# Walking the columns of matmuls in other orders, in five stages of an encoder trunk

## The chip, the cores and the metric

The kernel runs on one core of one Trainium2 chip. The metric is the device time of one execution in microseconds. It runs as one program that covers two whole layers and the final norm.

## The reference

Two layers of an encoder on a sequence of 512 tokens with 1024 features, in float32. Each layer mixes tokens in three branches, merges them, and then does a SwiGLU feed-forward and a gated per-layer embedding:

```python
for i in range(DEPTH):
    h = rmsnorm(x, mix_norm[i])
    z = h @ w_in[i]
    ...                      # recurrent branch, latent attention, forgetting attention
    merged = g[:, :, 0] * y_a + g[:, :, 1] * y_b + g[:, :, 2] * y_c
    x = x + merged @ w_o[i]
    hf = rmsnorm(x, ffn_norm[i]) @ w_gate_up[i]
    x = x + (jax.nn.silu(hf[..., :D_FF]) * hf[..., D_FF:]) @ w_down[i]
    pg = jax.nn.sigmoid(rmsnorm(x, ple_norm[i]) @ w_ple_gate[i])
    x = x + pg * (p[i] @ w_ple[i])
return rmsnorm(x, final_norm)
```

The parts that the change touches are the last three products of a layer: `w_gate_up` (1024 to 2 x 2816 features), `w_down` (2816 to 1024), and `w_ple` (256 to 1024) with `w_ple_gate` (1024 to 1024).

## The kernel before

Activations are kept feature-major: 128 features on the partitions, the 512 tokens along the columns. A dense product (`dense`, L246) takes one of the eight PSUM banks, 128 output features by 512 tokens of float32, and adds to it over k, the blocks of 128 input features. To keep float32 accuracy, weights and activations are each split in two float32r parts, hi and lo, and each k makes three matmuls (`mm3`, L239): hi x hi, hi x lo, lo x hi. The weights are the stationary operand, 128 x 128; the moving operand is a page of 512 tokens. All of it goes through `mm` (L236), whose `nc.tensor.matmul` is L237 of the profile. A page (`pr`) is 1024 contiguous columns per partition, hi in the first 512 and lo in the last; a bank is 512 contiguous columns. So each matmul of a dense product reads 512 neighbouring columns and adds to 512 neighbouring columns, first to last.

The weights come as a stream in the order of their use: 256 KB units of four tiles by DMA from SyncE, split by ScalarE (L112) and VectorE (L113) into a ring of five units (`hl`). When a product is done, VectorE and ScalarE read its bank whole and in order and give it back.

The feed-forward (`ffn`) runs 22 pairs of gate and up products, each 8 k blocks of three matmuls, 1056 matmuls in all; then 8 down products of 22 k blocks, 528 matmuls. The embedding (`ple`) runs 8 products of 2 k blocks and 8 of 8, 240 matmuls of 512 columns; in the second layer it ends in `ple_last`, whose gate products take 256 tokens at a time. A norm's 1/rms is summed by four one-column matmuls against a column of ones and spread over the partitions by two matmuls of 512 columns (`norm_bcast`, L332) that run among the first products of the next stage. `trunk` calls `mix`, `ffn` and `ple` for each layer. The order of the work is set by a scheduler, from the order of the code and the dependencies of tiles.

Of the kernel before, what the change touches and what calls it, by code (L numbers as in the profile page):

```python
# [26 lines left out]
# columns of w_in  # L27
# [3 lines left out]
# columns of the small per-partition vectors, per layer  # L31
V_MIX, V_FFN, V_PLE, V_GB, V_CW, V_CB, V_BA, V_BX, V_QN, V_KN, V_BF = (
    0, 8, 16, 24, 48, 64, 68, 72, 76, 79, 81)
NV = 82
V_LAM = DEPTH * NV          # lambdas of all layers, side by side
# [3 lines left out]
NUNITS = 606                # units of four 128x128 weight tiles in the stream  # L39
KEPT = NUNITS - 16          # from here on the stream is kept on chip: it is used twice  # L40
PACKED = (8, 9, 311, 312)  # units whose tiles hold the parts of 64 columns side by side


class Pages:
    """Pages of one tile, handed out oldest-freed first."""
# [39 lines left out]
class Stream:  # L85
    """The weights, in the order in which TensorE uses them: loaded ahead, split into two
    float32r parts that sum to the float32 value."""
# [46 lines left out]
    def tile(self, spec):  # L134
        """hi and lo of the next 128x128 tile"""
        u, k = divmod(self.pos, 4)
        if k == 0:
            self._ensure(u)
        self.spec.append(spec)
        self.pos += 1  # L140
        return self._parts(u, slice(128 * k, 128 * k + 128))

    def again(self, i):
        """tile i of the stream, one of those that were kept"""
        return self._parts(i // 4, slice(128 * (i % 4), 128 * (i % 4) + 128))
# [6 lines left out]
    def wide(self, spec):  # L152
        """hi and lo of a 128x512 tile, at the start of a unit"""
        self.align()
        u = self.pos // 4
        self._ensure(u)
        self.spec += [(spec, i) for i in range(4)]
        self.pos += 4
        return self._parts(u)

# [6 lines left out]
class Trunk:  # L167
    def __init__(self, ctx, tc, wst, vec, xT, pT, trig, masks, outT, last):
        self.tc, self.nc = tc, tc.nc
        self.a_vec, self.a_x, self.a_p, self.a_trig, self.a_masks, self.a_out, self.a_last = (  # L170
            vec, xT, pT, trig, masks, outT, last)
        nc = self.nc
        pool = ctx.enter_context(tc.tile_pool(name="sb", bufs=1))
        ps = ctx.enter_context(tc.tile_pool(name="ps", bufs=1, space=bass.MemoryType.PSUM))
        dr = ctx.enter_context(tc.tile_pool(name="dr", bufs=1, space=bass.MemoryType.DRAM))
        NR, NF, NRAW, NHL = 31, 20, 4, 5
        raw = pool.tile([128, NRAW * 512], F32, name="raw")
        hl = pool.tile([128, NHL * 1024], F32R, name="hl")
        self.w = Stream(tc, wst, raw, hl, NRAW, NHL)
        self.pr = Pages(pool.tile([128, NR * 1024], F32R, name="pr"), NR, 1024, "float32r")  # L180
        self.w.pages = self.pr
        self.raw = raw
        self.pf = Pages(pool.tile([128, NF * 512], F32, name="pf"), NF, 512, "float32")
        self.tmp = self.pf
        self.banks = Banks([ps.tile([128, 512], F32, name=f"bank{i}") for i in range(8)])
        self.pth = pool.tile([128, 1664], F32R, name="pth")
        self.ptl = pool.tile([128, 1664], F32R, name="ptl")
        self.identr = pool.tile([128, 128], F32R, name="identr")
        self.ident = self.identr[:, :].bitcast(F32)
        self.fmask = pool.tile([128, 128], F32, name="fmask")  # L190
        self.onesr = pool.tile([128, 128], F32R, name="onesr")
        self.one = pool.tile([128, 2], F32, name="one")
        self.eps = pool.tile([128, 2], F32, name="eps")
        self.vec = pool.tile([128, NVEC], F32, name="vec")
        self.sp = pool.tile([128, DEPTH * 4], F32, name="sp")
        self.msp = pool.tile([128, DEPTH * 4], F32, name="msp")
        self.small = pool.tile([128, 96], F32, name="small")
        self.xs = dr.tile([KD, 128, SEQ], F32, name="xs")
        self.chunk = dr.tile([4, 2 * SEQ], F32R, name="chunk")
        self.small_at = 0  # L200
        self.defer = None

    # -- small things ---------------------------------------------------------------------

    def cols(self, n):
        """n columns of a ring of small per-partition values"""
        if self.small_at + n > 96:
            self.small_at = 0
        s = self.small_at
        self.small_at += n  # L210
        return self.small[:, s:s + n]
# [24 lines left out]
    def mm(self, out, a, b, start, stop):  # L236
        self.nc.tensor.matmul(out, a, b, start=start, stop=stop, skip_group_check=True)  # L237
# [6 lines left out]
    # -- products, as generators that stop after every k tile -----------------------------  # L244

    def dense(self, spec, xs, evac, m=128):  # L246
        """out[m, tokens] = sum over k of W[k, m] * X[k, tokens]; xs are pages"""
# [11 lines left out]
    def group(self, specs, xs, evacs):  # L259
        """several of them side by side, k tile by k tile"""  # L260
# [20 lines left out]
    # -- RMSNorm ---------------------------------------------------------------------------  # L281

    def norm_add(self, st, x):
        """adds the squares of x (128 features) to the sums of norm st"""
# [17 lines left out]
    def norm_sum(self, st, n, fold=None):  # L302
        """token-major 1/rms, times fold, and its diagonal for the broadcast"""
# [10 lines left out]
        # 1/sqrt(v): a first value from the bits of v, good to 2e-3, and three Newton steps  # L314
# [30 lines left out]
    def normed(self, x, g):  # L345
        """page with both parts of x * g"""
        p = self.pr.take()
        self.ts(p.h, x, g)
        self.stt(p.l, x, g, p.h.bitcast(F32), ALU.mult, ALU.subtract)
        return p  # L350

    def after_norm(self, st, n, gen, s1, s2):
        """the first products after a norm, whose results wait for it; the sums are taken after
        s1 of their steps and the broadcast after s2"""
# [11 lines left out]
    # -- set-up -----------------------------------------------------------------------------  # L366

    def log1p_exp_neg(self, out, t1, t2, u, e):
        """out = log1p(s) / 2 with s = exp(-|u|), as atanh(y) with y = s / (2 + s)"""
# [11 lines left out]
    def setup(self):  # L381
# [11 lines left out]
        # TensorE's clock rises while it is busy  # L393
# [30 lines left out]
        # softplus(-lambda), times 2  # L424
# [9 lines left out]
    # -- mixers -------------------------------------------------------------------------------  # L434
# [4 lines left out]
    def mix(self, layer):  # L439
# [6 lines left out]
        # recurrent branch  # L446
# [39 lines left out]
        # rotary key and forget logits  # L486
# [12 lines left out]
        def rope(z, src, out_h, out_l, m):  # L499
            """z may be src"""  # L500
# [8 lines left out]
        def key_and_forget():  # L509
            """the rotary key, and the sums of the log forget gates; both parts of the weights side  # L510
            by side, so that one pass serves both"""
# [33 lines left out]
        # attention pieces  # L545
        qp, kp = {}, {}

        def ev_heads(pages, p, r, fox, is_q):
            """two heads' queries or keys to their pages, times 1/rms unless r is None"""
            f8 = 0.125 if fox and is_q else 1.0  # L550

            def f(b):
# [21 lines left out]
                for e in range(2):  # L574
# [3 lines left out]
                    if fox:  # L578
                        # queries [hi, hi | lo, extra], keys [hi, lo | hi, extra] or [lo, hi | hi, extra]
# [26 lines left out]
        def values(spec, X, rT):  # L606
            """token-major values: page per token tile, [head][hi 64 | lo 64]"""
# [23 lines left out]
        # recurrence: gates, then the scan  # L631
# [32 lines left out]
        def lru_tail():  # L664
            # one change of ScalarE's tables for all of them
# [23 lines left out]
        def renorm(*ks):  # L689
            """x * g / rms, for the products from here on"""  # L690
# [17 lines left out]
        # merge  # L708
# [39 lines left out]
        # attention  # L748
        def attention(fox, odd, plan, tail):
            """plan[p]: products (with their count of k tiles) to run beside head pair p; tail: a  # L750
            generator that runs beside the last steps"""
# [118 lines left out]
        # second phase products: latent projections  # L870
# [60 lines left out]
        def place_rope(p):  # L931
            """after the pair's pages are there"""
# [47 lines left out]
        # latent attention  # L980
# [24 lines left out]
        # output projection, residual, next norm  # L1005
# [22 lines left out]
    def ffn(self, layer):  # L1028
# [36 lines left out]
        self.st, self.xp = {}, []  # L1065

# [70 lines left out]
    def ple_last(self, X, pw):  # L1137
        """the last of them, and the final norm, by halves of the tokens"""
# [32 lines left out]
        def finish(js):  # L1171
            """the first half, by features"""
# [12 lines left out]
        def turn(j, x):  # L1185
            """the second half, by tokens: x times the final gain, to be transposed, and the squares"""
# [70 lines left out]
@with_exitstack  # L1257
def trunk(ctx, tc, *aps):
    t = Trunk(ctx, tc, *aps)
    t.setup()  # L1260
    for layer in range(DEPTH):
        t.mix(layer)
        t.ffn(layer)
        t.ple(layer)
    assert (t.w.pos + 7) // 8 * 2 == NUNITS, f"the stream has {t.w.pos} tiles"
    return t


# [85 lines left out]
def _masks():  # L1354
    """the causal mask of a diagonal block; and the chunk mask as a product of rank 4: row r is one
    for the queries in the first half of token tile r, and -1e30 for the keys in its second half"""
# [33 lines left out]
```

## Time and profile before

| | us |
|---|---|
| median of 2 runs | 1826.52 |
| the runs | 1824.92 and 1828.12 |
| span of the profiled execution, first to last instruction | 1825.0 |
| TensorE busy | 1807.5 |
| VectorE busy | 1210.6 |
| ScalarE busy | 817.1 |

The profiled execution's time is its span and the little that lies around it; the span stands 1.5 us under the median of the runs. Matmuls are pipelined, so the duration of one (392 ns in the mean) is longer than the distance between the starts of two, and busy TensorE time is not a measure of its rate; the rate is read from starts. In the names of the profile, `bank` is PSUM, `pr` are pages of two float32r parts, `pf` pages of float32, `hl` the split weights, `onesr` and `one` constants. PE is TensorE, DVE is VectorE, ACT is ScalarE.

### The profile page before, as it was taken

To read this page: it belongs to the slowest core of one execution; us is meant where nothing else is said; L and a number is where in the kernel's file an instruction comes from. 1 tells how busy PE (TensorE), PEld (TensorE's weight loads), DVE (VectorE), ACT (ScalarE), POOL (GpSimd) and SP (SyncE) were. 2 spreads that over 40 slices of the span, in tenths; PEclk is the share of its full clock that TensorE was granted. 3 is DMA by queue.
4 is the path that set the end of the run, shared out by engine and by line. 5 is a ranking of instruction groups with operands and counts; after the bars stand their busy time and mean duration, and the time that the engine had idled before them with its cause. 6 is when DMAs were issued, how large, how long until landed. Compare 5 with 4: busy or idle time off the path is not lost. (4 is left out here: it accounts for less than half of the span.)

```text
span 1825.0 us, 24155 instructions
## 1 busy us (share of the span) xinstructions
PE 1807.5 (99%) x8490; PEld 1505.6 (82%) x8490; DVE 1210.6 (66%) x2421; ACT 817.1 (45%) x1562; POOL 117.2 (6%) x234
## 2 busy tenths in 40 slices
PE   9999999999999999999999999999999999999998
PEld 8778888888888888888887788888888888888887
DVE  8997678866665555444778966888576555553457
ACT  4766556553333333223447655565533333332243
POOL 1220001100000000000103200010000000000000
PEclk9999999999999999999999999999999999999999
DMA  5232223324222222322333322242232222232231
GB/s 178 91 131 82 81 78 117 97 72 139 96 95 96 96 98 98 110 94 97 133 110 122 106 81 82 91 116 85 87 128 92 99 98 97 95 109 99 98 116 47
DMA packets 98826, 184.17 MB, mean 101 GB/s; under 512 B 13552, under 2 KB 14752, under 8 KB 98704
## 3 DMA queue, kind: packets, MB, share of 16 engines
q1 hardware_dynamic: 89280, 162.04, 25.7%
q0 software_dynamic: 8416, 19.45, 3.8%
q8 instruction: 66, 1.08, 0.2%
q10 hardware_dynamic: 1008, 1.14, 0.2%
q14 instruction: 56, 0.46, 0.1%
HBM read 173.98 MB, written 4.21 MB: 98 GB/s over the span
## 5 line engine op out<-in xcount | busy, mean ns | idle before, releaser
L237 PE MATMUL bank<-pr,hl 128*128 128x512 f32 (+1 forms) x6812 | 1602.9, 392 | 2.8 <-ACT pr L233 1.1
L237 PEld LDWEIGHTS bank<-pr,hl 128*128 128x128 f32 (+1 forms) x6812 | 1269.9, 188 | 267.3 <-ACT pr L233 2.0
L112 ACT CAST hl<-raw 128x512 fp32r<-128x512 f32 x590 | 364.3, 618 | 672.0 <-PE bank L237 403.8
L113 DVE TENSOR_TENSOR hl<-raw,hl 128x512 fp32r<-128x512 f32 x590 | 404.2, 686 | 378.6 <-ACT hl L112 360.4
L221 DVE TENSOR_TENSOR pf<-pf 128x512 f32<-128x512 f32 (+3 forms) x235 | 151.1, 651 | 31.8 <-ACT pf L230 29.9
L221 DVE TENSOR_TENSOR pf<-bank,pf 128x512 f32<-128x512 f32 (+3 forms) x198 | 132.8, 676 | 58.6 <-PE bank L237 32.1
L230 ACT ACTIVATE pf<-pf 128x512 f32<-128x512 f32 (+1 forms) x145 | 86.1, 600 | 112.7 <-DVE pf L221 110.5
L237 PE MATMUL bank<-pr 128*128 128x256 f32 (+5 forms) x704 | 120.7, 303 | 4.1 <-ACT pf L230 2.2
L237 PEld LDWEIGHTS bank<-pr 128*128 128x128 f32 (+1 forms) x704 | 102.7, 191 | 14.1 <-ACT pf L230 2.7
L221 DVE TENSOR_TENSOR pr<-pf,pr 128x512 fp32r<-128x512 f32 (+2 forms) x126 | 85.6, 682 | 4.5 <-ACT pr L233 3.5
L230 ACT ACTIVATE pf<-bank,small 128x384 f32<-128x384 f32 (+3 forms) x130 | 68.9, 531 | 38.5 <-DVE small L836 35.4
L233 ACT CAST pr<-pf 128x512 fp32r<-128x512 f32 (+1 forms) x114 | 70.4, 620 | 33.2 <-DVE pf L218 23.1
L853 ACT CAST pth<-bank 128x128 fp32r<-128x128 f32 (+3 forms) x128 | 54.0, 427 | 58.7 <-PE bank L828 50.5
L221 DVE TENSOR_TENSOR ptl<-bank,pth 128x128 fp32r<-128x128 f32 (+3 forms) x128 | 61.7, 485 | 13.9 <-ACT pth L853 9.9
L836 DVE TENSOR_REDUCE small<-bank 128x1 f32<-128x384 f32 (+3 forms) x128 | 61.6, 484 | 7.6 <-PE bank L237 6.5
L237 PE MATMUL bank<-hl,pr 128*128 128x512 f32 x240 | 56.3, 391 | 0.4 <-DVE hl L113 0.4
L828 PE MATMUL bank<-identr,pf 128*128 128x128 f32 x320 | 55.0, 273 | 0.0
L237 PEld LDWEIGHTS bank<-hl,pr 128*128 128x128 f32 x240 | 44.7, 188 | 10.3 <-DVE hl L113 1.1
L225 DVE TENSOR_SCALAR pf<-pf,small 128x384 f32<-128x384 f32 (+3 forms) x128 | 48.6, 383 | 2.6
L828 PEld LDWEIGHTS bank<-identr,pf 128*128 128x128 f32 x320 | 40.2, 140 | 8.3
L218 DVE SCALAR_TENSOR_TENSOR pf<-pf,bank 128x512 f32<-128x512 f32 x48 | 32.6, 683 | 21.6 <-PE bank L237 21.2
L230 ACT ACTIVATE pf<-bank,vec 128x512 f32<-128x512 f32 x60 | 40.9, 689 | 12.9 <-PE bank L237 12.5
(112 smaller groups left out, 796.6 us busy)
## 6 DMA issues: line engine op xcount, KB each, us to landing
raw<-wst SPq DMA_DIRECT2D x606, 256.0 KB, 2.6
pf<-xT POOLq DMA_DIRECT2D x16, 256.0 KB, 3.3
pr<-pr POOLq DMA_DIRECT2D x32, 128.0 KB, 2.6
pf<-xs POOLq DMA_DIRECT2D x16, 256.0 KB, 3.2
pf<-trig POOLq DMA_DIRECT2D x12, 256.0 KB, 3.1
pf<-xT SPq DMA_DIRECT2D x8, 256.0 KB, 5.3
xs<-pf POOLq DMA_DIRECT2D x8, 256.0 KB, 2.7
pf<-pT POOLq DMA_DIRECT2D x4, 256.0 KB, 3.1
```

Of the source, the lines that this page charges most:

```text
L112: self.nc.scalar.copy(hi, src)
L113: self.nc.vector.tensor_tensor(lo, src, hi.bitcast(F32), op=ALU.subtract)
L218: self.nc.vector.scalar_tensor_tensor(out, a, s, b, op0=op0, op1=op1)
L221: self.nc.vector.tensor_tensor(out, a, b, op=op)
L225: self.nc.vector.tensor_scalar(out, a, s1, None, op0=op0)
L230: return self.nc.scalar.activation(out, a, f, **kw)
L233: self.nc.scalar.copy(hi, src)
L237: self.nc.tensor.matmul(out, a, b, start=start, stop=stop, skip_group_check=True)
L828: nc.tensor.transpose(T[:, c], p2.ap[:, c], self.ident[:, :])
L836: nc.vector.reduce_max(R[t][:, 0:1], S[:, :m], axis=AX.X, negate=True)
L853: self.nc.scalar.copy(hi, src)
```

## The change

`mm` gets a walk: a rearrangement that it applies both to the moving operand and to the output, where the moving operand has 512 columns and no inner structure. The column of the page that is multiplied and the column of the bank that is added to stay the same pair; only the order in which the instruction goes through the 512 pairs is another one. `trunk` sets one walk for each stage:

- layer 0, gate/up: `p (a c b) -> p c a b` with a=2, b=16: 16 columns of the first half, the same 16 of the second half, the next 16 of the first, and so on;
- layer 0, down: the same with b=2: two columns from each half in turn;
- layer 0, embedding: a=8, b=2: two columns from each eighth (64 columns) in turn;
- layer 1, gate/up: a=2, b=8: eight columns from each half in turn;
- layer 1, down: `p (c a b) -> p a c b` with a=2, b=16: the even runs of 16 columns, then the odd ones;
- layer 1, embedding, and both `mix` stages: none.

The stationary operand is not touched, nor are the evacuations of the banks. Comments and docstrings are dropped as well, and the numbers of lines shift (L237 becomes L250).

```diff
+def by(pattern, **sizes):
+    return lambda ap: ap.rearrange(pattern, **sizes)
+
+WALKS = (by("p (a c b) -> p c a b", a=2, b=16), by("p (a c b) -> p c a b", a=2, b=2),
+         by("p (a c b) -> p c a b", a=8, b=2), by("p (a c b) -> p c a b", a=2, b=8),
+         by("p (c a b) -> p a c b", a=2, b=16), None)
...
+        self.walk = None
...
     def mm(self, out, a, b, start, stop):
+        if self.walk is not None and b.shape[-1] == SEQ and len(b.shape) == 2:
+            out, b = self.walk(out), self.walk(b)
         self.nc.tensor.matmul(out, a, b, start=start, stop=stop, skip_group_check=True)
...
     def ffn(self, layer):
...
         self.st, self.xp = {}, []
+
+        self.walk = WALKS[3 * L + 1]
...
     for layer in range(DEPTH):
         t.mix(layer)
+        t.walk = WALKS[3 * layer]
         t.ffn(layer)
+        t.walk = WALKS[3 * layer + 2]
         t.ple(layer)
+        t.walk = None
```

The instructions of TensorE at the beginning of layer 0's gate/up products, before; `one` is the norm's sum and `onesr` its broadcast, and a row's end gives the shape of the moving operand and a count:

```order
L237 MATMUL bank_72<-pr,hl 128x512
L237 MATMUL bank_74<-one,pf 128x1 x4
L237 MATMUL bank_72<-pr,hl 128x512 x16
L237 MATMUL bank_67<-pr,hl 128x512 x23
L237 MATMUL bank_68<-pr,onesr 128x512
L237 MATMUL bank_67<-pr,hl 128x512
```

And the same place on TensorE after:

```order
L250 MATMUL bank_72<-pr,hl 128x16x2x16
L250 MATMUL bank_74<-one,pf 128x1 x4
L250 MATMUL bank_72<-pr,hl 128x16x2x16 x16
L250 MATMUL bank_67<-pr,hl 128x16x2x16 x23
L250 MATMUL bank_68<-pr,onesr 128x16x2x16
L250 MATMUL bank_67<-pr,hl 128x16x2x16
```

The instructions, their banks and their order are the same; the 512 columns have become 16 times 2 times 16, and the broadcast's two matmuls are walked as well. The second place is on TensorE where layer 0's down products end and those of the embedding begin, before:

```order
L237 MATMUL bank_67<-pr,hl 128x512 x66
L237 MATMUL bank_70<-pr,hl 128x512 x66
L237 MATMUL bank_69<-pr,hl 128x512 x6
L237 MATMUL bank_71<-pr,hl 128x512 x6
L237 MATMUL bank_74<-pr,hl 128x512 x6
```

On TensorE after, at this place:

```order
L250 MATMUL bank_67<-pr,hl 128x128x2x2 x66
L250 MATMUL bank_70<-pr,hl 128x128x2x2 x66
L250 MATMUL bank_69<-pr,hl 128x32x8x2 x6
L250 MATMUL bank_71<-pr,hl 128x32x8x2 x6
L250 MATMUL bank_74<-pr,hl 128x32x8x2 x6
```

Nothing moved here either: a down product is 66 matmuls in runs of two from halves, an embedding product 6 in runs of two from eighths. On the other engines the order of instructions and their waits are the same before and after, but for the numbers of lines.

## The prediction

> **What bounds the kernel now.** I read the profile's page first: the busy shares, the granted clock, the chain that ended last and the costliest groups.
>
> ```profile
> span 1825.0 us, 24155 instructions
> ...
> PE 1807.5 (99%) x8490; PEld 1505.6 (82%) x8490; DVE 1210.6 (66%) x2421; ACT 817.1 (45%) x1562; POOL 117.2 (6%) x234
> ...
> PEclk9999999999999999999999999999999999999999
> ...
> PE 43%; DVE 2%; issue 0%; ACT 0%; DMA 0%; DVEq 0%; ACTq 0%; POOLq 0%
> ...
> L237 PE MATMUL bank<-pr,hl 128*128 128x512 f32 (+1 forms) x6812 | 1602.9, 392 | 2.8 <-ACT pr L233 1.1
> ```
>
> TensorE is busy for 99% of the span at full granted clock, and its main group of 6812 products was idle for 2.8 us in all before them. Nothing feeds it late. Next I cut out the five stages that the change touches, by their times on TensorE: layer 0's gate/up, down and embedding products, then layer 1's gate/up and down products. The columns are the stretch, its length, then busy time (and count) of TensorE, its weight loads, VectorE, ScalarE and GpSimd, the granted clock, the DMA share and GB/s.
>
> ```profile
> 494.80:735.40 240.60, 240.60 (x1067) 199.34 (x1066) 136.66 (x219) 79.83 (x134) 0.54 (x1) 1.00 0.28 98
> 735.40:855.10 119.70, 119.70 (x530) 99.12 (x529) 49.40 (x77) 33.13 (x54) 1.06 (x2) 1.00 0.29 100
> 855.10:913.00 57.90, 57.90 (x261) 48.06 (x260) 42.26 (x85) 26.48 (x45) 6.45 (x12) 1.00 0.36 124
> 1393.20:1633.60 240.40, 240.40 (x1066) 199.18 (x1065) 136.39 (x219) 79.70 (x134) 0.54 (x1) 1.00 0.28 97
> 1633.60:1753.30 119.70, 119.70 (x530) 99.12 (x529) 50.71 (x79) 34.77 (x57) 0.54 (x1) 1.00 0.30 103
> ```
>
> In all five TensorE is busy from end to end, the clock is 1.00, and VectorE, the next engine, is busy for 41 to 73% of the stretch. So the time of these stages is the number of their matmuls times the distance between two starts, and nothing else. That distance is read from the timeline of TensorE, whose rows give a start, a duration, and how many instructions were merged:
>
> ```profile
> 1411.33 353.31 PE L237 MATMUL bank<-pr,hl 128*128 128x512 f32 x1558
> 1764.47 5.92 PE L237 MATMUL bank<-pr 128*128 128x256 f32 x48
> ...
> 1779.02 18.27 PE L237 MATMUL bank<-pr 128*128 128x256 f32 x151
> 1797.13 0.50 PE L237 MATMUL bank<-one,pf 128*128 128x1 f32 x4
> ```
>
> From 1411.33 to the next row's 1764.47 there are 1558 matmuls of 512 columns: 353.14 / 1558 = 226.7 ns each. (The 392 ns of the page is one matmul from its start to its modelled end, and overlaps its neighbours.) From 1779.02 to 1797.13 there are 151 of 256 columns: 119.9 ns each. The difference, 106.8 ns for 256 columns, makes 0.417 ns per column, and 226.7 - 512 x 0.417 leaves 13.2 ns per matmul that does not depend on its columns.
>
> **The change part by part.** It adds and removes no instruction. The matmuls under a walk, with the lengths of contiguous runs that each now reads and writes: layer 0 gate/up 1056 and 2 of the norm's broadcast (32 runs of 16 columns), layer 0 down 528 (256 runs of 2, from halves), layer 0 embedding 240 and 2 (256 runs of 2, from eighths), layer 1 gate/up 1056 and 2 (64 runs of 8), layer 1 down 528 (32 runs of 16, all even ones and then all odd ones). That is 3414 matmuls. At 226.7 ns they fill 774 us, 42% of the span.
>
> Order on every engine, wait for wait, is unchanged, and the weights, their loads, the evacuations and the DMAs keep their contiguous forms. Moving operand and sums are permuted alike, so each sum still lands in its own column. Hence no wait is added or moved, and no queue is passed. What stays is one question: does a matmul whose 512 columns are read and written in runs still take 226.7 ns?
>
> The trace of before has no matmul that reads or writes in short runs; its moving operands and outputs are all contiguous. The nearest rows are of other engines, which do read banks and write pages in runs. These are groups of VectorE and then of ScalarE, with the mean ns of one after the busy time:
>
> ```profile
> L221 DVE TENSOR_TENSOR pf<-bank,pf 128x512 f32<-128x512 f32 x156 | 106.4, 688 | 38.1 <-PE bank L237 32.1 <-ACT pf L342 5.9
> ...
> L221 DVE TENSOR_TENSOR pr<-bank,pr 128x512 fp32r<-128x512 f32 x8 | 5.5, 683 | 0.1
> ```
>
> ```profile
> L853 ACT CAST pth<-bank 128x512 fp32r<-128x512 f32 x32 | 18.8, 588 | 25.8 <-PE bank L828 25.4
> ...
> L342 ACT COPY pf<-bank 128x512 f32<-128x512 f32 x10 | 5.9, 589 | 16.0 <-PE bank L237 15.9
> ...
> L233 ACT CAST pr<-bank 128x512 fp32r<-128x512 f32 x8 | 4.5, 596 | 0.0
> ```
>
> VectorE's 683 ns is the latent values' split, which writes its page in eight runs of 64 with gaps of 64; contiguous it is 688 ns. ScalarE writes the same runs in 596 ns, runs of 128 in 588, and contiguous pages in 589. So a jump costs VectorE nothing, and ScalarE at most (596 - 589) / 7 = 1 ns. Per jump of TensorE I take zero, the value of VectorE and of the 128-column runs; the ends are zero and 1 ns. Jumps per matmul are 31, 255, 255, 63 and 31, so there are 1058 x 31 + 528 x 255 + 242 x 255 + 1058 x 63 + 528 x 31 = 312,000 of them, and the dear end is 312 us. These rows cannot show the second thing that matters, that TensorE takes a column every 0.417 ns where VectorE takes (688 - 419) / 256, from its 256-column form below, or 1.05 ns: a memory that keeps up with VectorE in runs might not with TensorE.
>
> ```profile
> L221 DVE TENSOR_TENSOR pf<-pf 128x256 f32<-128x256 f32 x23 | 8.7, 419 | 0.8 <-ACT pf L230 0.5
> ```
>
> A gain is bounded too. The columns' 0.417 ns is the rate of full granted clock and cannot fall; only the 13.2 ns per matmul could, if they were a conflict of addresses at the seam of two matmuls: 3414 x 13.2 = 45 us. The Trainium skill, in "TensorE: Matmul & The Clock Gate", section "Back-to-back issue gap", has N / 2.4 + 2.5 ns for a warm matmul, some 216 ns at 512 columns; by that the gain would end at 3414 x 10.9 = 37 us. This trace disagrees with the page: 226.7 ns over 1558 in a row. The same 13.2 ns stands in matmuls of 512 and of 256 columns and so does not look like a conflict that the order of columns sets; I take no gain.
>
> The sum is made on the profiled execution: its span of 1825.0 us, plus 0. The two timed runs are 1824.92 and 1828.12, so the span lies 1.5 us under their median of 1826.5. Moved to that median, the forecast is 1826.5 us.
>
> If the forecast is wrong upward, nothing covers it: TensorE has no idle time in these stages to give, and the others already wait for it (waits in 494 to 913 us, with total, times and longest):
>
> ```profile
> ACT hl L112 <- PE bank L237: 141.6, 76, 3.0
> ...
> DVE pf L221 <- PE bank L237: 15.2, 49, 1.6
> ```
>
> **The rivals.** Each price is added to 1826.5.
>
> A, two columns are too few, and a run of 2 goes at half rate, while 8 and 16 are free. A memory that hands over four columns at a time would do that. The stages with runs of 2 hold 528 + 242 = 770 matmuls, each 512 x 0.417 = 213.5 ns longer: +164 us, 1991 us. It decides from the first matmul of layer 0's down products. Against it: with halves, the next run but one is the neighbour of this one, so that two open places would do. No row excludes it. Chance 0.08.
>
> B, only the eighths are slow: there eight places are open in turn before the next pair of the first comes. 242 x 213.5 ns = +52 us, 1878 us. With partial losses of the two-column stages up to this size, chance 0.10.
>
> C, each jump costs a column's time: 312,000 x 0.417 ns = +130 us, 1957 us. It would show as 13 ns on a matmul with 31 jumps and 106 ns on one with 255. The rows of VectorE speak against it. Chance 0.05.
>
> D, any departure from one contiguous run halves the rate in all five stages: 3414 x 213.5 ns = +729 us, 2555 us. The Trainium skill, "Advanced Engine Details and Errata", section "Memory Cachelines", says both that "any non-contiguous AP significantly slows down matmuls" in PSUM, which is this rival, and that every two consecutive elements should be contiguous for best throughput, which all five walks satisfy and which is my forecast. For SBUF it asks for at least two hits on a 16-byte line; a run of two float32 is just that. No run here shows which sentence holds. In runs of 16 a jump comes every 6.7 ns (16 x 0.417), and VectorE writes runs of 64 at full rate, which makes a loss of half unlikely. Chance 0.03.
>
> E, faster: the 13.2 ns go with the new order. 1826.5 - 45 = 1781 us. Chance 0.04.
>
> That the change does not reach the chip is excluded by the order of the changed kernel, where the operands' shapes differ in all 3414.
>
> **How the numbers follow.** The forecast has 0.70, and A to E 0.30. A difference under 2%, 37 us, is about what a measurement of this kernel can't be sure to tell from none, so 0.70 is the chance of "same"; A, B, C and D are slower, 0.26 together; E is faster by 2.5%, 0.04. Down, the range goes to 1822, a little more than the 3.2 us by which the two runs differ below the median. Up, it takes in B: 1880. It leaves out A, C, D and E, 0.20.
>
> **What would show it.** If I am right, the starts of TensorE's matmuls in each of the five stages are still 226.7 ns apart, and the stretches are still 240, 120, 58, 240 and 120 us long. A shows 440 ns in layer 0's down and embedding stages and 226.7 in the other three; B in the embedding stage alone; C shows 240, 333, 333, 253 and 240 ns in the order of the stages; D shows 440 in all; E shows about 213. My forecast would fall by any loss that grows with the number of runs or with the number of places they come from, which the busy share of TensorE would not show, since it is full already; only the distance of starts does.

## The result: 1981.6 us, 8.6% slower

The changed kernel took 1981.62 us in the median (1981.14 and 1982.09) against 1826.52: 1.0856 times the kernel before, 95% interval 1.0839 to 1.0873. The span grew from 1825.0 to 1978.9 us. These are the lines of the page that answer to those shown of before:

```profile
span 1978.9 us, 24155 instructions
...
PE 1961.2 (99%) x8490; PEld 1520.0 (77%) x8490; DVE 1212.0 (61%) x2421; ACT 817.0 (41%) x1562; POOL 117.2 (6%) x234
...
PEclk9999999999999999999999999999999999999999
...
L250 PE MATMUL bank<-pr,hl 128*128 128x512 f32 (+1 forms) x6812 | 1756.2, 417 | 3.0 <-ACT pr L244 1.2
```

The instructions, the clock and the idle time before the main group (3.0 us) are as before; VectorE and ScalarE work as long as before (1212 and 817 us). What grew is TensorE's own busy time, by 154 us; its weight loads show 14 us more, but they run beside the matmuls. The five stages, with the columns of the prediction's table:

```profile
492.40:746.70 254.30, 254.30 (x1066) 201.50 (x1065) 136.49 (x219) 79.60 (x134) 0.54 (x1) 1.00 0.28 92
746.70:919.30 172.60, 172.60 (x528) 102.51 (x527) 49.60 (x77) 33.29 (x54) 0.83 (x2) 1.00 0.21 69
919.30:1042.00 122.70, 122.70 (x267) 55.16 (x266) 45.10 (x87) 26.96 (x46) 7.17 (x14) 0.99 0.18 61
1522.60:1780.50 257.90, 257.90 (x1066) 202.08 (x1065) 136.47 (x219) 79.76 (x134) 0.54 (x1) 1.00 0.28 91
1780.50:1907.00 126.50, 126.50 (x529) 99.30 (x528) 50.54 (x79) 34.85 (x57) 0.54 (x1) 1.00 0.29 97
```

Against before they are longer by 13.7, 52.9, 64.8, 17.5 and 6.8 us, 155.7 us together. (The cuts do not hold quite the same matmuls: the third has 267 and had 261, so that its 64.8 us are some 2 us too many. The granted clock of 0.99 there is one stretch of 3.4 us, which comes up again further down.) Within each stage the starts of matmuls follow one another with great regularity, and their mean distance, which is used from here on, is:

| stage | walk | ns from start to start | over 226.7 |
|---|---|---|---|
| layer 0 gate/up | halves, runs of 16 | 240.0 | 13.3 |
| layer 0 down | halves, runs of 2 | 328.0 | 101.3 |
| layer 0 embedding | eighths, runs of 2 | 486.7 | 260.0 |
| layer 1 gate/up | halves, runs of 8 | 243.3 | 16.7 |
| layer 1 down | even, then odd runs of 16 | 240.0 | 13.3 |

With the counts of the prediction: 1058 x 13.3 + 528 x 101.3 + 242 x 260.0 + 1058 x 16.7 + 528 x 13.3 ns = 155 us. The medians of the runs lie 155.1 us apart, so the distances account for the whole loss.

### The profile page after: what moved, and what is told of

The parts are those of the page before. It is cut to its first block, busy times and chain, and to the rows that moved or that the text cites. A ratio compares the mean times of both kernels' runs of the same rounds, so it can differ in the third digit from the quotient of the medians.

```text
span 1978.9 us, 24155 instructions
## 1 busy us (share of the span) xinstructions
PE 1961.2 (99%) x8490; PEld 1520.0 (77%) x8490; DVE 1212.0 (61%) x2421; ACT 817.0 (41%) x1562; POOL 117.2 (6%) x234
## 5 line engine op out<-in xcount | busy, mean ns | idle before, releaser
L250 PE MATMUL bank<-pr,hl 128*128 128x512 f32 (+1 forms) x6812 | 1756.2, 417 | 3.0 <-ACT pr L244 1.2
L250 PEld LDWEIGHTS bank<-pr,hl 128*128 128x128 f32 (+1 forms) x6812 | 1284.3, 190 | 405.7 <-issue 66.2
L250 PE MATMUL bank<-pr 128*128 128x256 f32 (+5 forms) x704 | 120.4, 302 | 4.0 <-ACT pf L241 2.2
L250 PEld LDWEIGHTS bank<-pr 128*128 128x128 f32 (+1 forms) x704 | 102.5, 190 | 13.9 <-ACT pf L241 2.6
L250 PE MATMUL bank<-hl,pr 128*128 128x512 f32 x240 | 56.4, 391 | 0.6 <-DVE hl L113 0.6
L250 PEld LDWEIGHTS bank<-hl,pr 128*128 128x128 f32 x240 | 44.7, 188 | 10.5 <-DVE hl L113 1.3
L241 ACT ACTIVATE pf<-bank,vec 128x512 f32<-128x512 f32 x60 | 40.9, 689 | 13.2 <-PE bank L250 12.8
```

Source lines behind the costliest of these rows:

```text
L241: return self.nc.scalar.activation(out, a, f, **kw)
```

## The experiments

Since the trace shows a distance for each stage by itself, one kernel tries five walks; in the diffs a walk stands in words. Where not said otherwise, the stages, their counts and the rest of the kernel are those of the changed kernel.

### Which end pays: the read or the sums

The changed kernel, with one end of each matmul back in order:

```diff
 # reads walked
-            out, b = self.walk(out), self.walk(b)
+            b = self.walk(b)
 # sums walked
-            out, b = self.walk(out), self.walk(b)
+            out = self.walk(out)
```

> The walks are applied to the moving operand alone; the sums are written first to last, so that the tokens of a bank come out permuted in the five stages and the output is not the reference's. In the changed kernel the starts of the five stages are 240, 328, 487, 243 and 240 ns apart, against 226.7 contiguous. Theory 1, the jumps cost where TensorE reads its moving operand: the same five distances, some 1980 us in all. Theory 2, they cost where the sums are written: all five at 226.7 ns and 1826 us. If both ends pay and their losses add, each of the two kernels shows a part, and the parts sum to the whole; if the slower end sets the pace, one of the two shows the whole and the other less.

> The walks are applied to the sums alone; the moving operand is read first to last, so that the tokens of a bank come out permuted in the five stages and the output is not the reference's. Theory 1, the cost is in the reading of the moving operand: 226.7 ns in all five stages, 1826 us. Theory 2, the cost is in the writing of sums: 240, 328, 487, 243 and 240 ns, some 1980 us.

Reads walked: 1980.4 us. Sums walked: 1824.8 us, with 1828.3 for the kernel before on the same chip. On TensorE's timeline, the row that runs from the first norm's end through the rest of gate/up, the down products and the first embedding products of layer 0, and the 39 products after it; first with the reads walked:

```profile
512.24 444.10 PE L250 MATMUL bank<-pr,hl 128*128 128x512 f32 x1582
956.14 0.99 PE L250 MATMUL bank<-one,pf 128*128 128x1 f32 x8
956.99 19.29 PE L250 MATMUL bank<-pr,hl 128*128 128x512 f32 x39
```

And with the sums walked:

```profile
510.71 358.75 PE L250 MATMUL bank<-pr,hl 128*128 128x512 f32 x1582
869.30 0.95 PE L250 MATMUL bank<-one,pf 128*128 128x1 f32 x8
870.11 9.15 PE L250 MATMUL bank<-pr,hl 128*128 128x512 f32 x39
```

The same 1582 matmuls take 444 us and 359 us, the 39 in eighths 19.3 and 9.2 us. Stage by stage, the reads alone give 240.0, 328.0, 486.7, 243.3 and 240.0 ns, the changed kernel's five distances; the sums alone give 226.7 ns in all five. The whole loss lies in the reading of the moving operand, and the order in which sums are written costs nothing, down to runs of two columns from eighths. Theory 1 stands, theory 2 falls.

### Do the long runs cost by themselves?

```diff
-WALKS = (halves of 16, halves of 2, eighths of 2, halves of 8, even and odd runs of 16, None)
+WALKS = (halves of 16, None, None, halves of 8, even and odd runs of 16, None)
```

> The change without its two stages of two-column runs: layer 0 gate/up, layer 1 gate/up and layer 1 down keep their walks, layer 0 down and embedding go first to last. By the distances of the changed kernel the loss is 1058 x 13.3 + 1058 x 16.7 + 528 x 13.3 ns = 39 us, a time near 1865 us and a ratio of 1.021. If the two-column stages disturb the others, or these disturb them, less than that.

Measured: 1864.61 us against 1825.44, ratio 1.0216, interval 1.0197 to 1.0234, and 240.0, 226.7, 226.7, 243.3 and 240.0 ns in the stages. The three walks with long runs cost 39 us alone, as their distances say, and the stages do not act on one another.

### Run length and number of places

Both ends walked, in other sizes:

```diff
+WALKS = (halves of 4, halves of 32, halves of 2, eighths of 16, eighths of 8, None)
```

> Both ends walked, other sizes: layer 0 gate/up halves in runs of 4 (128 runs), down halves in runs of 32 (16 runs), embedding halves in runs of 2 (256 runs), layer 1 gate/up eighths in runs of 16 (32 runs), down eighths in runs of 8 (64 runs). Theory a, a run costs about a column's time (0.417 ns), whatever it comes from, and the embedding's 487 ns are of something else: 280, 233, 328, 240 and 244 to 253 ns. Theory b, a jump among eight places costs more than one among two (in the changed kernel 2.4 columns' times against 1): 280, 233, 328, then 259 and 292 ns. If the embedding stage of halves shows 487 ns too, it is the stage and not the eighths that is slow.

Measured: 250.0, 236.7, 333.3, 239.6 and 234.1 ns, 1899.1 us. Halves of 2 in the embedding stage take 333 and not 487, so it is the eighths that are slow there, not the stage. (Why they take 333 there and 328 among the down products is not shown.) But neither theory holds for the rest. Halves of 4 have 128 runs and lose 23.3 ns, where a column's time for each would be 53. Eighths of 8 lose less (7.4 ns) than halves of 8 (16.7 ns) and than eighths of 16 (12.9). A price per jump does not describe it.

With the reads alone walked, shorter runs and single sweeps:

```diff
+            b = self.walk(b)
 # strides
+WALKS = (every 2nd column, 2 of every 4, every 4th, 2 of every 8, every 8th, None)
 # places
+WALKS = (quarters of 2, sixteenths of 2, thirty-seconds of 2, eighths of 4, halves of 1, None)
```

> The moving operand alone is walked, the sums are written first to last, so that tokens come out permuted and the output is not the reference's. One sweep over the page per phase: layer 0 gate/up every 2nd column (2 sweeps), down 2 of every 4 columns (2 sweeps), embedding every 4th column (4 sweeps), layer 1 gate/up 2 of every 8 (4 sweeps), down every 8th (8 sweeps). Theory lines, what costs is a 4-column line (16 bytes) from which fewer than two columns are taken at a time: 226.7, 226.7, slow, 226.7, slow. Theory blocks, what costs is each visit to another block of about 16 columns: 64, 64, 128, 128 and 256 visits, which by the halves in runs of 8, 4 and 2 are some 243, 243, 250, 250 and 328 ns. Theory jumps, a column's time for each jump: 440, 333, 440, 333, 440 ns.

> The moving operand alone is walked, the sums are written first to last, so that tokens come out permuted and the output is not the reference's. Runs taken in turn from several places: layer 0 gate/up quarters in runs of 2, down sixteenths (32 columns apart) in runs of 2, embedding thirty-seconds (16 columns apart) in runs of 2, layer 1 gate/up eighths in runs of 4, down halves in runs of 1. Known: halves in runs of 2 take 328 to 333 ns, eighths in runs of 2 take 487, halves in runs of 4 take 250. Theory places, each further open place adds to the cost: quarters between 328 and 487, sixteenths and thirty-seconds at or above 487. Theory blocks, each visit to another block of 16 columns costs the same, however many places are open: all of the first three alike, 256 visits, so either 328 or 487; halves of 1 with 512 visits twice the loss of halves of 2, 430 to 440 ns or more; eighths in runs of 4, 128 visits, 250. Theory distance, the loss depends on how far apart the places are, as places that fall on one bank of the memory would: the three differ from one another without order.

Strides: 451.1, 451.1, 460.0, 461.4 and 431.1 ns. All are near 440, so the theories of lines and of blocks fall, and the theory of jumps misses the second and fourth (333 expected). Places: 443.3, 461.3, 431.1, 278.1 and 215.8 ns. More places do not mean more loss (eighths are slower than thirty-seconds), so the theories of places and of blocks fall too; the theory of distance is not excluded by these three. And the last stage does what none had foreseen: halves in runs of **one** column, 511 jumps in a matmul, are 10.8 ns *faster* than first to last.

### The fast order

```diff
+            b = self.walk(b)
 # singles
+WALKS = (quarters of 1, eighths of 1, sixteenths of 1, thirty-seconds of 1, halves of 1, None)
 # pairs: one column from each of two neighbouring blocks of this many columns in turn
+WALKS = (blocks of 128, of 64, of 16, of 8, of 4, None)
```

> The moving operand alone is walked, the sums are written first to last, so that tokens come out permuted and the output is not the reference's. Runs of one column, in turn from quarters, eighths, sixteenths, thirty-seconds (layer 0 gate/up, down, embedding, layer 1 gate/up) and from halves once more (layer 1 down). Halves in ones took 215.8 ns against 226.7 first to last, halves in twos 328. Theory pair, two columns are fetched at once and the fetch goes at full rate when the second lies at a fixed distance in the same position of another line, for two places alone: 216 for halves, about 440 for all others. Theory lines, a line stays open while its columns are taken in turn and some number of lines can be open: quarters near 216 too, and the loss begins at the number of places that is too many.

> The moving operand alone is walked, the sums are written first to last, so that tokens come out permuted and the output is not the reference's. Runs of one column taken in turn from two places, as halves in ones, but the two places lie nearer: 128 columns apart (layer 0 gate/up), 64 (down), 16 (embedding), 8 (layer 1 gate/up), 4 (layer 1 down). Theory pair or lines, the distance does not matter as long as it is another line: 216 ns in all five, some more where blocks are short. Theory distance, places that fall on the same bank of the memory disturb one another: the five differ, and the near ones are the slow ones or the fast ones.

Singles: 283.3, 486.7, 435.0, 433.3 and again 215.8 ns. Pairs: 215.8 in all five stages, whatever the distance, and 1789.9 us for the whole kernel. Two places in ones are fast, four lose 57 ns, eight and more are near half the rate. Quarters at 283 lie between the two theories' values. The theory of distance falls for two places in ones; nothing nearer than 4 columns was tried. The row of the 1582 matmuls, here by pairs 128 columns apart, then 64 and 16:

```profile
512.23 341.61 PE L253 MATMUL bank<-pr,hl 128*128 128x512 f32 x1582
853.67 0.95 PE L253 MATMUL bank<-one,pf 128*128 128x1 f32 x8
```

From start to start that is (853.67 - 512.23) / 1582 = 215.8 ns.

Is the fast read a true one? In this kernel the output is the reference's: VectorE and ScalarE deal the tokens of a page into its halves, and TensorE reads them back by halves in ones, so that the sums come first to last.

```diff
+    def deal(self, page):
+        return page.rearrange("p (a c) -> p c a", a=2) if self.dealt else page
+    def flat(self, x):
+        return x.rearrange("p (c a) -> p c a", a=2) if self.dealt else x
...
-            self.split(p.h, p.l, u.ap)
+            self.split(self.deal(p.h), self.deal(p.l), self.flat(u.ap))
...
-            self.mm3(b[:m], wh[:, :m], wl[:, :m], x.h, x.l, k == 0, k == n - 1)
+            h, l = (x.h, x.l) if not x.dealt else (y.rearrange("p (a c) -> p c a", a=2) for y in (x.h, x.l))
+            self.mm3(b[:m], wh[:, :m], wl[:, :m], h, l, k == 0, k == n - 1)
```

> The kernel before, with one thing changed in the same five stages: VectorE and ScalarE store a page's even tokens in its first half and the odd ones in the second, and TensorE reads it by halves in ones, so that the tokens reach the sums in their natural order and the sums are written first to last. The output is the reference's. If 215.8 ns of halves in ones is the time of a true read, 3408 matmuls gain 10.8 ns each, 37 us: near 1789 us, ratio 0.980. If the walked read was fast only because it fetched something else, the values would show it. If the writing of pages with jumps makes VectorE or ScalarE late, TensorE shows idle time before its matmuls in these stages and the gain is smaller.

Measured: 1788.57 us against 1825.11, ratio 0.9798, interval 0.9781 to 0.9814. The row of the 1582 matmuls on TensorE's timeline, and two stretches of gate/up and down products of layer 0 in the columns of the stages' table:

```profile
510.11 341.61 PE L246 MATMUL bank<-pr,hl 128*128 128x512 f32 x1582
851.55 0.95 PE L246 MATMUL bank<-one,pf 128*128 128x1 f32 x8
```

```profile
520.00:720.00 200.00, 200.00 (x928) 175.13 (x928) 127.55 (x176) 78.04 (x116) 0.54 (x1) 1.00 0.31 103
760.00:840.00 80.00, 80.00 (x372) 70.04 (x372) 39.43 (x56) 24.43 (x41) 1.03 (x2) 1.00 0.31 101
```

(851.55 - 510.11) / 1582 = 215.8 ns. TensorE stays busy throughout, VectorE is busy for 64% of the first stretch (the whole stage had 57% before). The fast read is a true read, and the 37 us come in full.

The same for the pages of the mixing stages that serve only as a moving operand:

```diff
...
-                self.split(p.h, p.l, t.ap)
+                self.split_dealt(p, t.ap)
...
```

> As the kernel with dealt pages in the five stages, and in the mixing stages too, for the pages that serve only as a moving operand (the renormed input, the branches' results, the merged pages, the query latent): even tokens in a page's first half, odd ones in the second, read by halves in ones, sums first to last. The output is the reference's. 1302 more matmuls per layer gain 10.8 ns, 28 us on top of the 37: near 1760 us, ratio 0.964, if TensorE stays the bound there. If ScalarE and VectorE, busy for about 60 and 75% in the mixing stages, become late by their jumping writes, less.

Measured: 1765.31 us against 1825.06, ratio 0.9672, interval 0.9656 to 0.9688: the fastest kernel of this study, 5 us short of what was expected. The price is in the page's span and engine shares, first of the kernel that deals five stages, then of this one:

```profile
span 1786.1 us, 24155 instructions
...
PE 1768.5 (99%) x8490; PEld 1508.4 (84%) x8490; DVE 1245.2 (70%) x2421; ACT 839.6 (47%) x1562; POOL 117.4 (7%) x234
```

```profile
span 1763.8 us, 24156 instructions
...
PE 1740.1 (99%) x8490; PEld 1513.1 (86%) x8490; DVE 1265.1 (72%) x2421; ACT 855.3 (48%) x1562; POOL 117.5 (7%) x234
```

Its groups of TensorE, ScalarE and VectorE:

```profile
L251 PE MATMUL bank<-pr,hl 128*128 128x512 f32 x6796 | 1532.9, 383 | 6.9 <-DVE hl L114 3.5 <-ACT pr L247 1.8 <-DVE pf L235 0.8
...
L247 ACT CAST pr<-pf 128x512 fp32r<-128x512 f32 x110 | 114.7, 1048 | 32.4 <-DVE pf L232 20.8 <-DVE pf L235 8.0 <-DMA pf<-pT 2.5
L235 DVE TENSOR_TENSOR pr<-pf,pr 128x512 fp32r<-128x512 f32 x110 | 114.0, 1041 | 22.7 <-ACT pr L247 21.8 <-issue 0.3
```

The means, 1048 ns of ScalarE and 1041 of VectorE, mix two kinds: by the shapes that the trace keeps, 92 of the 110 pages are dealt, and they take 1133 and 1112 ns, while the other 18 are still written first to last, in 617 and 681. The same two groups of the kernel before, where all pages were written first to last, show:

```profile
L221 DVE TENSOR_TENSOR pr<-pf,pr 128x512 fp32r<-128x512 f32 x110 | 74.8, 682 | 3.9 <-ACT pr L233 3.5 <-issue 0.2
...
L233 ACT CAST pr<-pf 128x512 fp32r<-128x512 f32 x110 | 67.9, 620 | 31.5 <-DVE pf L218 23.1 <-DVE pf L221 5.3 <-DMA pf<-pT 2.2
```

VectorE and ScalarE are a little fuller over the span, and TensorE's main group waits 6.9 us in all, 3.5 of them for VectorE's weights. TensorE's busy time fell by the 28 us that were expected. But TensorE is idle for 1763.8 - 1740.1 = 23.7 us of this span, against 1786.1 - 1768.5 = 17.6 of the kernel that deals five stages; these 6 us are about what is missing.

### What are the 10.8 ns?

Two attempts. The first makes the weights narrower, the second makes very few jumps.

```diff
 # narrow: layer 0 first to last with 64, 32, 96 weight columns; layer 1 by pairs with 64 and 32
+            m, w = self.walk
+            a, out = a[:, :m], out[:m]
+            b = b if w is None else w(b)
 # few jumps, reads alone
+WALKS = (halves of 64, halves of 128, second half before the first, pairs on lo pages, even and odd runs of 4, None)
```

> Only the first 64 (layer 0 gate/up and layer 1 gate/up), 32 (layer 0 down, layer 1 down) or 96 (layer 0 embedding) of the 128 output features are computed in the five stages, so the stationary operand is narrower and the output is not the reference's. Layer 0 reads first to last, layer 1 reads each page by pairs 8 columns apart. A matmul of 512 columns took 226.7 ns first to last and 215.8 by pairs, and 512 columns alone are 213.3. Theory weights, the 10.8 ns that the pairs save are reads of the next weights that get in the way of the moving operand's: with fewer weight columns the first-to-last stages fall towards 215.8, to some 221, 218.5 and 224 ns. Theory start, they belong to the beginning of a contiguous read: 226.7 in all three stages of layer 0. By both, the pairs stay at 215.8.

> The moving operand alone is walked, the sums are written first to last, so that tokens come out permuted and the output is not the reference's. Layer 0 gate/up: halves in runs of 64 (8 runs), down: halves in runs of 128 (4 runs), embedding: the second half before the first (2 runs), layer 1 gate/up: only the middle one of each three matmuls, the one on the page's lo part, by pairs 8 columns apart, down: the even runs of 4 columns, then the odd ones. Known over 226.7 ns: 16 runs of halves +10.0, 32 runs +13.3, 64 runs +16.7, 128 runs +23.3. Theory run, some part of each run is lost at its start, less the shorter the run: 8 runs, 4 runs and 2 runs give at most +7, +5 and +3. Theory matmul, a walk costs a lump per matmul once it jumps at all: near +7 in all three. Layer 1 gate/up: if the gain belongs to the walked matmul's own read, a third of 10.8 ns, 223.1 in the mean; if it needs the neighbours to be walked too, nearer to 226.7. Layer 1 down: a half of the columns of every 8 is skipped in each sweep, 128 runs; by the number of runs 250, by the stride, as 2 of every 4 columns had it, 440 to 460.

Narrow: 230.0, 231.7 and 230.0 ns first to last, 215.8 ns by pairs. Fewer weight columns do not shorten the distance, they lengthen it by 3 to 5 ns, and it is no longer one number: with 64 columns the distances go round through 236, 229, 224, 227, 234 and 230. So the 10.8 ns are not a time that grows with the weights read. The theory of a start says 226.7 in all, which is not met either; what sets them is left open.

Few jumps: 226.7, 226.7 and 226.7 ns, then 224.5 and 231.1. Halves in runs of 64 and more cost nothing, so neither theory's lump is there; the loss begins between runs of 64 and of 32. Of three matmuls with the middle one by pairs, the distances are 215, 232 and 227, beginning with the middle one: it is short by its own read, whatever its neighbours, but the contiguous one after it takes 5 ns longer, so that the mean gains 2.2 of the 3.6 ns expected. Neither forecast of the mean, 223.1 or 226.7, is met. Even and odd runs of 4 lose 4.4 ns, where 2 of every 4 lose 224: the expectation by the stride was wrong, and that by the number of runs (250) was too high. The row of the 1582 matmuls, in halves of 64, halves of 128 and the second half first, shows (868.56 - 509.98) / 1582 = 226.7 ns:

```profile
509.98 358.75 PE L252 MATMUL bank<-pr,hl 128*128 128x512 f32 x1582
868.56 0.95 PE L252 MATMUL bank<-one,pf 128*128 128x1 f32 x8
```

The traces hold one more piece of evidence, which no run was made for: in some stretches of 3.4 us the granted clock is 0.5. The changed kernel has two of them between its first and its last products, one among the eighths of layer 0's embedding and one among contiguous matmuls of layer 1's mixing stage (the granted clock is the first number after the last bracket):

```profile
957.00:960.30 3.30, 3.30 (x8) 2.18 (x7) 1.47 (x7) 0.63 (x1) 0.00 (x0) 0.51 0.00 0
1151.60:1154.60 3.00, 3.00 (x8) 2.31 (x7) 2.97 (x7) 1.43 (x5) 2.94 (x6) 0.50 0.46 151
```

In the second, starts are 427 ns apart, which is 512 columns at twice 0.417 ns and nothing over: the 13 ns are gone. Dealt pages in such a stretch (129.9 us of the last dealt kernel) take 427 ns as well. In the first, the eighths stay at 487 ns, as at full clock; in the same way sixteenths and thirty-seconds in ones stay at 435 and 433, and every 2nd column goes from 451 to 454. So the slow reads do not keep time with TensorE's clock, and the remainder of a contiguous read is not a lump that is added to the columns' time. Both look like a supply of columns that is slower than TensorE at full clock; what limits it in a contiguous read stays open.

## Why the prediction was wrong

**What held.** The work is the same, instruction by instruction and wait by wait; TensorE is the bound and has nothing to cover a loss; the distance of starts is the quantity that shows it. The sum's form, matmuls times distance, gives 155 us of the measured 155 once the measured distances are put in.

**The step that failed** is "Per jump of TensorE I take zero, the value of VectorE and of the 128-column runs". It was a rate from other engines, in runs of 64 and 128 columns, carried over to runs of 2, 8 and 16. In fact halves in runs of 64 and 128 cost TensorE nothing as well; the measured loss of halves is 10.0 ns a matmul at runs of 32, 13.3 at 16, 16.7 at 8, 23.3 at 4 and 101 at 2, and that of eighths in runs of 2 is 260. All of it is lost in reading the moving operand, and a price per jump, of whatever size, does not describe it. The prediction named the weak point, that TensorE takes a column in 0.417 ns where VectorE takes 1.05, and gave it too little weight: the likeliest case had 0.70 on the strength of rows that did not bear on it. The dear end, 1 ns per jump and 312 us, did hold the truth. The range did not, as 1880 took in the eighths alone. Nor is 2% "about what a measurement of this kernel can't be sure to tell from none": the interval of the result is 0.34% wide.

**The rivals.** A's price for the two-column stages was 164 us and they lost 116 (53 + 63), so its 1991 us came near the time by luck: its reason, half rate for runs of 2 and no loss for longer ones, is not what happened. Halves lost 101 ns and not 213, eighths 260, and the long runs 39 us. C gave 240, 333, 333, 253 and 240 ns, right within 10 ns in four stages of five, and 1957 us; had the walks been only those, it would have passed for the truth. The run with other lengths showed that it is not: 128 runs of 4 lose less than half of C's price. B was right that eighths are slower than halves, and wrong that halves are free. D did not happen: the long runs lost 6 to 7%. E was no outcome of these walks, but its claim is true: of the 13.2 ns that do not depend on the number of columns, another order takes 10.8 away. Whether a conflict at the seam of two matmuls is the reason, as the prediction supposed, is not shown. The argument against E, that a remainder equal in 256 and in 512 columns does not come from their order, was wrong.

**Rule and trace.** In the Trainium skill, in "Advanced Engine Details and Errata", "Memory Cachelines", neither sentence on PSUM speaks of what decides here. "Any non-contiguous AP significantly slows down matmuls" does not agree with the sums walked alone: 226.7 ns in all five stages. That two consecutive elements suffice there does agree, for these walks. The sentence on SBUF, two hits on a 16-byte line to absorb the latency, does not hold for this float32r read: every 2nd column, and 2 of every 4, have two hits a line and take 451 ns. In the Trainium skill, in "TensorE: Matmul & The Clock Gate", "Back-to-back issue gap", N / 2.4 + 2.5, given there for a warm matmul by itself, makes 215.8 ns for 512 columns. The trace has this to the tenth when pages are read by pairs, in a stream of matmuls, and misses it by 10.8 ns when they are read first to last; the 37 us by which the prediction bounded a gain in that sentence are what the dealt pages of the five stages gained.

## What to carry to other kernels

An order of columns that is free on one engine, or in runs of 64, says nothing of TensorE's moving operand in shorter runs: where TensorE is the bound, a moving operand like this one is laid out so that it is read in runs of 64 or more, or else in ones from two places, and a rearrangement is put into the writing of sums, which was free here. A steady remainder per instruction, like the 13 ns here, is worth one experiment on access patterns even when it looks fixed; it was worth 3.3% of this kernel. Where the trace has no row for the very thing that is changed, the range has to reach to the dear end of the bound.

## What the runs showed of the hardware

All distances of a 512-column float32r matmul, in ns from start to start, by the order of the moving operand; the sums' order made no difference where both were tried.

| taken in turn from | runs of 1 | 2 | 4 | 8 | 16 | 32 | 64, 128 |
|---|---|---|---|---|---|---|---|
| halves | 215.8 | 328 to 333 | 250.0 | 243.3 | 240.0 | 236.7 | 226.7 |
| quarters | 283.3 | 443.3 | | | | | |
| eighths | 486.7 | 486.7 | 278.1 | 234.1 | 239.6 | | |
| sixteenths | 435.0 | 461.3 | | | | | |
| thirty-seconds | 433.3 | 431.1 | | | | | |

Single sweeps: every 2nd column 451.1, 2 of 4 451.1, every 4th 460.0, 2 of 8 461.4, every 8th 431.1; but 4 of 8 231.1, and 16 of 32 240.0. First to last 226.7.

Two things stand out. Where columns come in whole groups of four, 16 bytes of float32, the loss was at most 51 ns. Where a group of four is not taken whole, the time goes to 430 to 490 ns, some 0.9 ns a column, about twice the 0.417, except where two places (or four, in ones) take turns: halves of 1 lose nothing, quarters of 1 and halves of 2 lie between. This looks like a memory line of 16 bytes of which two can be held open, but that is argued from these numbers and not shown (no run shifted a group of four by a column or two), and it does not explain why eighths of 8 are faster than halves of 8, nor why two places in ones beat a contiguous read. What the 10.8 ns of a contiguous read are stays open: they do not shrink with narrower weights, a few long jumps do not remove them, and at half the granted clock they are hidden. ScalarE and VectorE, too, pay for dealing single columns by turns to two halves: 1133 and 1112 ns a page against 620 and 682, where VectorE also reads the first part by turns.
